# Stick-breaking and dilated scores: the second query tile as three rounded float32r terms, and the stick-breaking work moved along the projection chunks

## The chip, the cores and the metric

The kernel runs on one core of a Trainium2 chip. The metric is the time of one execution on the device in microseconds; the median of three runs before the change is 249.99 us (249.98 to 250.0). A core has TensorE (matmuls; PE in the profile, PEld its weight loads), VectorE (DVE), ScalarE (ACT), GpSimd (POOL) and SyncE (SP), each with its own instruction queue that it works off in order, 16 DMA engines, the on-chip memory SBUF, and PSUM, eight banks into which TensorE writes. GpSimd cannot read PSUM.

## The reference, cut to what matters

Two layers of a decoder trunk, over 256 positions (two tiles of 128) of width 1024. Each layer normalises x, projects it to ten groups of columns, runs three branches over heads of width 64, gates them, and adds the output projection to x:

```python
hn = rms_norm(x, norm_gain)
proj = einsum('bsd,de->bse', hn, w_in)
a_q, a_k, a_v, a_g, b_x, b_g, c_q, c_k, c_v, c_g = split(proj)
qa, ka = rope(a_q), rope(a_k)                    # 8 heads
y_a = dilated_attention(qa, ka, va) * silu(a_g)
y_b = rg_lru_branch(b_x, ...) * silu(b_g)        # conv of width 4, then a gated recurrence
y_c = stick_breaking_attention(qc, kc, vc) * silu(c_g)   # 4 heads
x = x + einsum('bse,ed->bsd', concat([y_a, y_b, y_c]), w_out)
```

Dilated attention takes the causal scores q.k, weights them by how many of three (window, dilation) patterns hold a key, and applies a softmax. Stick-breaking takes z = q.k/8 under a strict causal mask, and weighs key s by sigmoid(z_s) times the product of sigmoid(-z_j) over the keys j between s and the query. Both need, per head, the scores of query tile 0 against keys 0 to 127 and of query tile 1 against keys 0 to 255. All is float32, and the output is compared in float32.

## The kernel before, in words

**Precision.** Projections are done in three terms. Each float32 operand is split into a rounded high part (type float32r) and a low part, the difference, also rounded; the product is high.high + low.high + high.low, with three float32r matmuls. The weights arrive by DMA in chunks (`load_chunk`, L101 to L111): per chunk two transfers on SP's queue, four ScalarE copies that round (L109), four VectorE subtracts that give the low part (L110). Scores, in contrast, are plain float32 matmuls before the change (L443 for stick-breaking, L497 for dilated), which TensorE works off as two records (passes) each.

**Order.** TensorE's order is the order of the program text (`manual_schedule` for TensorE). On the other engines a planner decides at build time in which order each queue holds its instructions; it goes by dependencies, the program order as priority, and its own estimate of times. Chunks are asked for `AHEAD` = 2 chunks in front of the one in use, 1 where the chunk has work placed in its middle, with the second then asked for behind that work (`proj_b`, L314 to L346).

The projection chunks that matter run in this order in each layer: CQ, CK (stick-breaking q and k), AQ0, AK0 (dilated q and k of heads 0 to 3), BX (recurrence input), AQ1, AK1 (dilated heads 4 to 7), CG (stick-breaking gate), BG, AG. A chunk is two halves of 128 output columns. In layer 0 each half is 24 matmuls of 256 columns (L211). In layer 1 the chunks CQ to AK1 are "paired": 8 matmuls of 512 columns that carry high and low part of x at once (L332) and 8 of 256 (L329), and ScalarE and VectorE then add the two halves of the result (L335, L337).

Other work is placed between halves, by the argument `mid` of `proj_b`. Before the change:

- mid AQ0: the stick-breaking scores (`sb_scores`, L436), then on ScalarE two sigmoids per head, on VectorE two scans and a product per head (L454, L456);
- behind AQ0 and AK0: their results are rotated (`rotate`, L476: four VectorE instructions each) into the tiles q0 and k0;
- mid BX and behind BX: the 12 transposes of the stick-breaking weights (`turned`, L458 to L464), one bank and then two; behind BX also the convolution on VectorE and two small DMAs on GpSimd's queue (L549);
- mid AQ1: the first dilated scores (`dil_scores(0)`, L489) and their softmax: VectorE masks and takes the extreme value (L504), ScalarE exponentiates (L514), VectorE divides (L517);
- behind CG: the transposes of those probabilities; mid BG: the recurrence's gate matmuls (L557), both products with v (L427) and the second dilated scores (`dil_scores(4)`).

**Buffers.** Scores and transposes share four PSUM banks (`at`), projections three (`pp`). A head of 64 lies on partitions 0 to 63 or 64 to 127, so heads come in pairs that use different rows of TensorE's array. The SBUF tiles named yh0, yl0 (first half of the gated outputs, split), ag (dilated gate) and q0 have one buffer each: a new use waits until all readers of the last one are done. GpSimd does little: memsets of a column of the stick-breaking weights (L452), small scalars, two DMAs per layer.

Of the kernel before, what the change touches and what calls it, by code (L numbers as in the profile page):

```python
# [9 lines left out]
F32 = mybir.dt.float32  # L10
# [38 lines left out]
def trunk_kernel(ctx: ExitStack, tc: tile.TileContext, x, first_x, first, wpack, prm_d, gatew, gains, consts, rope, out):  # L49
# [247 lines left out]
    for l in range(L):  # L297
# [7 lines left out]

        y_half(0)

        def proj_a(ps, w, t, kb, nk, cw, first, last):
# [125 lines left out]
        halves = ((0, slice(0, 128)), (1, slice(128, 384)))  # L434

        def sb_scores():  # L436
            for p in (0, 2):
                for h in (p, p + 1):
                    zs[h] = bank(at, "s")
                for t, cs in halves:  # L440
                    for h in (p, p + 1):
                        hr, hb, _ = head(h)
                        pe.matmul(zs[h][:, cs], qc[hr, hb, t * P:(t + 1) * P], kc[hr, hb, 0:(t + 1) * P],  # L443
                                  start=t == 0, stop=True, skip_group_check=True)
            table(SIGM, [split[l, CH_AK[0]]])
            for h in range(NHC):
                z = zs[h][:, 0:384]
                bt, om = scr(384), scr(384)
                tab(om, z, AF.Sigmoid, scale=-1.0)
                tab(bt, z, AF.Sigmoid)  # L450
                w = sw[h] = wk.tile([P, 384], F32, name="sw", tag="sw", bufs=4)
                gps.memset(w[:, 127::256], 0.0)  # L452
                for lo, n in ((0, 127), (128, 255)):
                    dve.tensor_tensor_scan(w[:, lo:lo + n][:, ::-1], om[:, lo + 1:lo + 1 + n][:, ::-1],  # L454
                                           diag[:, 255 - n:255][:, ::-1], 0.0, ALU.mult, ALU.add)
                dve.tensor_mul(w, bt, w)  # L456
# [32 lines left out]
        def dil_scores(h0):  # L489
            sps = {}  # L490
            for p in (h0, h0 + 2):
                for h in (p, p + 1):
                    sps[h] = bank(at, "s")
                for t, cs in halves:
                    for h in (p, p + 1):
                        hr, hb, _ = head(h - h0)
                        pe.matmul(sps[h][:, cs], qT[h0][hr, hb, t * P:(t + 1) * P], kT[h0][hr, hb, 0:(t + 1) * P],  # L497
                                  start=True, stop=True)
            shifted = {}
            for h in range(h0, h0 + 4):  # L500
                xs = scr(384)
                mn = wk.tile([P, 2], F32, name="mn", tag="mn", bufs=4)
                for t, cs in halves:
                    dve.tensor_tensor_reduce(xs[:, cs], sps[h][:, cs], nmask[:, cs], -0.125, 3e38,  # L504
                                             ALU.add, ALU.min, mn[:, t:t + 1])
# [30 lines left out]
        bg = sb.tile([P, 2, S], F32, name="bg", tag="bg")  # L536
        ag = sb.tile([P, 4, S], F32, name="ag", tag="ag")
        cg = sb.tile([P, 2, S], F32, name="cg", tag="cg")
# [87 lines left out]
        emit_y(rt, bg, 0, 2)  # L626
        dil_softmax(y_c["s"])
        ps = proj_b(CH_AG)
        table(SIGM)
# [146 lines left out]
```

## Time and profile before

| | |
|---|---|
| median of three runs | 249.99 us (249.98 to 250.0) |
| the profiled execution's own time | 248.82 us |
| its span, first to last instruction | 246.7 us |
| granted TensorE clock | 0.996 |
| busy: TensorE, VectorE, ScalarE, GpSimd | 97%, 80%, 68%, 5% of the span |
| float32 score matmuls, records of 256 columns (L443 and L497) | 16 and 32, 377 ns each |
| float32 score matmuls, records of 128 columns | 16 and 32, 296 and 297 ns each |
| projection matmuls, float32r, 256 columns (L211, input whi) | 480, 285 ns each |

A row of a group reads: line, engine, operation, output<-inputs, shape, count, then busy time and the mean duration of one in ns, then idle time before them and what ended it. A record's duration holds its pipeline latency too; what one record costs in a stream is the distance from start to start. A row of the chain or of a timeline begins with the start and the length in us from the start of the span; a timeline row can hold a run of several instructions, with their count.

### The profile page before, as it was taken

What the parts mean: (1) busy time and instruction counts of PE and PEld (TensorE: products, weight loads), DVE (VectorE), ACT (ScalarE), POOL (GpSimd) and SP (SyncE); (2) the same over time, 40 slices, a digit from 0 to 9 for tenths busy, and PEclk for the clock granted to TensorE, in tenths of its full rate; (3) what the DMA queues carried; (4) which work ended last, traced back from release to release, by engine and by line L of the source; (5) the groups of instructions that cost most, each with busy time, mean ns of one, the idle gap of its engine ahead of it and who ended that gap; (6) DMA issues with size and microseconds to landing.
All of it is one profiled execution on the core that took longest, in us unless ns stands there. A gap on an engine that the chain in (4) does not pass through costs nothing.

```text
span 246.7 us, 4531 instructions
## 1 busy us (share of the span) xinstructions
PE 239.0 (97%) x1657; PEld 212.1 (86%) x1657; DVE 196.5 (80%) x442; ACT 167.2 (68%) x360; POOL 12.1 (5%) x45
## 2 busy tenths in 40 slices
PE   8999999999999999999999999999999999999990
PEld 4889999999998899878889988889889889987870
DVE  3885699999999799985792766999999987985253
ACT  3778989735947499964662885865498649992142
POOL 0037000001000000000100000000010000000000
PEclk9999999999999999999999999999999999999998
DMA  6989889268447741277157486605553672000022
GB/s 201 404 292 403 342 288 333 96 215 268 134 157 255 258 117 56 85 240 284 74 189 232 142 268 243 200 7 165 161 157 119 197 262 98 0 0 3 0 85 85
DMA packets 13173, 43.89 MB, mean 178 GB/s; under 512 B 1632, under 2 KB 2144, under 8 KB 13152
## 3 DMA queue, kind: packets, MB, share of 16 engines
q1 hardware_dynamic: 12384, 42.30, 51.1%
q10 hardware_dynamic: 576, 0.79, 0.9%
q0 software_dynamic: 192, 0.52, 0.7%
q8 instruction: 13, 0.21, 0.4%
q14 instruction: 8, 0.07, 0.1%
HBM read 42.03 MB, written 1.05 MB: 175 GB/s over the span
## 4 chain that ended last, share of the span: by engine, by line
PE 94%; DMA 2%; DVE 1%; ACT 1%; SPq 0%; issue 0%; ACTq 0%
PE pp L211 51%; PE pp L332 11%; PE s L211 9%; PE pp L329 5%; PE s L169 4%; PE s L463 3%; PE s L497 2%; PE y L427 2%; DMA st<-first 2%; PE pp L169 2%; PE s L443 1%; PE pp L427 1%; PE s L557 1%; PE s L259 1%; DVE xres L668 0%; ACT scr L242 0%
## 5 line engine op out<-in xcount | busy, mean ns | idle before, releaser
L110 DVE TENSOR_TENSOR wlo<-st,whi 128x512 fp32r<-128x512 f32 x132 | 84.1, 683 | 12.8 <-ACT whi L109 12.5
L109 ACT ACTIVATE whi<-st 128x512 fp32r<-128x512 f32 x132 | 73.9, 629 | 28.0 <-PE pp L211 11.8
L211 PE MATMUL pp<-xx,whi 128*128 128x256 f32 x480 | 63.3, 285 | 0.0
L211 PEld LDWEIGHTS pp<-xx,whi 128*128 128x128 f32 x480 | 59.7, 191 | 1.4 <-issue 1.3
L211 PE MATMUL pp<-xx,wlo 128*128 128x256 f32 x240 | 33.7, 283 | 0.0
L211 PEld LDWEIGHTS pp<-xx,wlo 128*128 128x128 f32 x240 | 30.9, 192 | 0.0
L332 PE MATMUL pp<-xx,whi 128*128 128x512 f32 x112 | 29.3, 396 | 0.0
L332 PEld LDWEIGHTS pp<-xx,whi 128*128 128x128 f32 x112 | 20.1, 189 | 4.1 <-ACT scr L83 0.3
L77 ACT ACT_TABLE_LOAD x13 | 16.7, 1283 | 1.9 <-PEq L769 1.7
L83 ACT ACTIVATE pr<-scr,mn 128x128 f32<-128x128 f32 (+1 forms) x32 | 14.1, 442 | 5.2 <-DVE mn L504 5.2
L329 PEld LDWEIGHTS pp<-xx,wlo 128*128 128x128 f32 x112 | 15.3, 190 | 1.1
L329 PE MATMUL pp<-xx,wlo 128*128 128x256 f32 x112 | 15.6, 282 | 0.0
L211 PE MATMUL pp<-whi,yh 128*128 128x512 f32 x48 | 14.5, 403 | 0.0
L211 PE MATMUL pp<-wlo,yh 128*128 128x512 f32 x48 | 14.0, 393 | 0.0
L211 PE MATMUL pp<-whi,yl 128*128 128x512 f32 x48 | 14.0, 393 | 0.0
L335 ACT ACTIVATE low<-pp 128x256 f32<-128x256 f32 x14 | 5.3, 382 | 9.1 <-PE pp L332 6.8
L211 PEld LDWEIGHTS pp<-wlo,yh 128*128 128x128 f32 x48 | 9.0, 188 | 2.1
L211 PEld LDWEIGHTS pp<-whi,yl 128*128 128x128 f32 x48 | 9.0, 188 | 2.0
L211 PEld LDWEIGHTS pp<-whi,yh 128*128 128x128 f32 x48 | 8.6, 188 | 2.0 <-issue 0.3
L169 PE MATMUL s<-whi,xx 128*128 128x512 f32 (+1 forms) x36 | 10.2, 404 | 0.1
L415 ACT ACTIVATE yh<-scr 128x512 fp32r<-128x512 f32 x8 | 5.0, 631 | 7.7 <-DVE scr L413 7.6
L504 DVE CUSTOM_DVE_ANT_0 scr<-s,con 128x128 f32<-128x128 f32 (+1 forms) x32 | 9.2, 351 | 0.0
(165 smaller groups left out, 355.2 us busy)
## 6 DMA issues: line engine op xcount, KB each, us to landing
st<-w_pack SPq DMA_DIRECT2D x66, 512.0 KB, 5.4
st<-first SPq DMA_DIRECT2D x7, 512.0 KB, 6.2
xres<-x_in SPq DMA_DIRECT2D x2, 512.0 KB, 8.1
gw_t<-gate_w SPq DMA_DIRECT2D x2, 256.0 KB, 6.9
gn<-gains SPq DMA_DIRECT2D x1, 512.0 KB, 6.7
xs<-xc POOLq DMA_DIRECT2D x4, 128.0 KB, 3.7
gf<-gains SPq DMA_DIRECT2D x1, 512.0 KB, 6.8
out<-scr SPq DMA_DIRECT2D x2, 256.0 KB, 2.1
```

What stands on the lines that cost most here:

```text
L77: load = act.preload_act_table_set(name)
L83: i = dep(act.activation(*a, **k), loaded["load"])
L109: split[l, c] = act.activation(hi[:, ws], st[:, ss], AF.Copy)
L110: dve.tensor_sub(lo[:, ws], st[:, ss], hi[:, ws].bitcast(F32))
L169: pe.matmul(ps[t][:, c0 - base:c1 - base], a[:, k, t * P:(t + 1) * P], b[:, c0:c1], start=k == 0 and i == 0 and c0 == base, stop=k == NK - ...
L211: pe.matmul(ps, a(k), b(k), start=first and i == 0, stop=last and i == len(seq) - 1)
L329: pe.matmul(ps[:, 0:S], lo[:, k, cs], xh[:, k, :], start=False, stop=False, skip_group_check=True)
L332: pe.matmul(ps, hi[:, k, cs], xx[:, k].rearrange("p h t -> p (h t)"), start=i == 0, stop=i == len(seq) - 1, skip_group_check=True)
L335: act.activation(low, ps[:, S:2 * S], AF.Copy, scale=sc)
L427: pe.matmul(y[hr, p * 128 + o:p * 128 + 256], vt[:, s0, hs], wts[i][s0], start=s0 == 0, stop=s0 == 1)
L463: pe.transpose(tp[:, i * P:(i + 1) * P], tiles[h0 + h][:, j * P:(j + 1) * P], ident)
L504: dve.tensor_tensor_reduce(xs[:, cs], sps[h][:, cs], nmask[:, cs], -0.125, 3e38, ALU.add, ALU.min, mn[:, t:t + 1])
```

## The change: what it does

For query tile 1 of all score groups, the float32 matmul is replaced by three float32r matmuls over rounded parts: q high . k high, q low . k high, q high . k low, summed in PSUM. Query tile 0 stays float32. A new function `split_keys` makes the parts: for q's second tile a copy that rounds and a subtract on GpSimd; for k over all 256 keys a copy on ScalarE (on GpSimd for heads 4 to 7) and a subtract on GpSimd. The parts live in the tiles yh0 and yl0 (stick-breaking, then heads 0 to 3) and ag and q0 (heads 4 to 7), so the gated outputs' first half and the gate tile are allocated later. A new function `scores` issues the matmuls, for each pair of heads: tile 0, then the three terms.

The stick-breaking scores move from the middle of AQ0 to the middle of AK0, their transposes from the middle and end of BX to the middle and end of AK1. BX has nothing in its middle any more. In layer 1 the first dilated scores move from the middle of AQ1 to its end; in layer 0 they stay.

```diff
-        y_half(0)
-
+        exact = {}
+
+        def split_keys(h0, q, k, tags):
+            parts = []
+            for full, tag, n in ((q[:, :, P:S], tags[1], P), (k, tags[0], S)):
+                both = sb.tile([P, 2, 2, n], F32R, name="qk3", tag=tag)
+                hi, lo = both[:, 0], both[:, 1]
+                if n == S and h0 != 4:
+                    act.activation(hi, full, AF.Copy)
+                else:
+                    gps.tensor_copy(hi, full)
+                gps.tensor_sub(lo, full, hi.bitcast(F32))
+                parts.append((hi, lo))
+            (qh, ql), (kh, kl) = parts
+            exact[h0] = (qh, kh), (ql, kh), (qh, kl)
+
+        def scores(ps, h0, q, k, p):
+            for n, (a, b) in enumerate(((q, k), *exact[h0])):
+                cs = slice(0, P) if n == 0 else slice(P, 384)
+                for h in (p, p + 1):
+                    hr, hb, _ = head(h)
+                    pe.matmul(ps[h][:, cs], a[hr, hb, 0:P], b[hr, hb, 0:P if n == 0 else S],
+                              start=n < 2, stop=n in (0, 3), skip_group_check=True)
+
         def sb_scores():
...
-                for t, cs in halves:
-                    for h in (p, p + 1):
-                        hr, hb, _ = head(h)
-                        pe.matmul(zs[h][:, cs], qc[hr, hb, t * P:(t + 1) * P], kc[hr, hb, 0:(t + 1) * P],
-                                  start=t == 0, stop=True, skip_group_check=True)
+                scores(zs, "sb", qc, kc, p)
...
         def dil_scores(h0):
...
-                for t, cs in halves:
-                    for h in (p, p + 1):
-                        hr, hb, _ = head(h - h0)
-                        pe.matmul(sps[h][:, cs], qT[h0][hr, hb, t * P:(t + 1) * P], kT[h0][hr, hb, 0:(t + 1) * P],
-                                  start=True, stop=True)
+                scores(sps, h0, qT[h0], kT[h0], p)
...
-        ag = sb.tile([P, 4, S], F32, name="ag", tag="ag")
...
             proj_to(kc, CH_CK)
+        split_keys("sb", qc, kc, ("yh0", "yl0"))
...
-        rotate(proj_b(CH_AQ[0], sb_scores), qT, 0, "q0")
-        rotate(proj_b(CH_AK[0]), kT, 0, "k0")
-        sw_t, sw_heads = turned_tile()
-        conv(lambda: turned(sw, 0, (0,), sw_t))
-        turned(sw, 0, (1, 2), sw_t)
+        rotate(proj_b(CH_AQ[0]), qT, 0, "q0")
+        rotate(proj_b(CH_AK[0], sb_scores), kT, 0, "k0")
+        split_keys(0, qT[0], kT[0], ("yh0", "yl0"))
+        conv(None)
...
-        rotate(proj_b(CH_AQ[1], second), qT, 4, "q1")
-        rotate(proj_b(CH_AK[1]), kT, 4, "k1")
+        q1_ps = proj_b(CH_AQ[1], second if l == 0 else None)
+        if l > 0:
+            second()
+        rotate(q1_ps, qT, 4, "q1")
+        sw_t, sw_heads = turned_tile()
+        rotate(proj_b(CH_AK[1], lambda: turned(sw, 0, (0,), sw_t)), kT, 4, "k1")
+        turned(sw, 0, (1, 2), sw_t)
+        split_keys(4, qT[4], kT[4], ("ag", "q0"))
...
         silu(cg, cg_ps)
 
+
+        y_half(0)
...
         dil_softmax(y_c["s"])
+        ag = sb.tile([P, 4, S], F32, name="ag", tag="ag")
         ps = proj_b(CH_AG)
```

More of the change, by code (lines that the diff above doesn't have):

```diff
@@ L490, in dil_scores @@
             sps = {}
-            for p in (h0, h0 + 2):
+            for p in (0, 2):
                 for h in (p, p + 1):
                     sps[h] = bank(at, "s")
-                for t, cs in halves:
-                    for h in (p, p + 1):
-                        hr, hb, _ = head(h - h0)
-                        pe.matmul(sps[h][:, cs], qT[h0][hr, hb, t * P:(t + 1) * P], kT[h0][hr, hb, 0:(t + 1) * P],
-                                  start=True, stop=True)
+                scores(sps, h0, qT[h0], kT[h0], p)
             shifted = {}
@@ L503, in dil_scores @@
                 for t, cs in halves:
-                    dve.tensor_tensor_reduce(xs[:, cs], sps[h][:, cs], nmask[:, cs], -0.125, 3e38,
+                    dve.tensor_tensor_reduce(xs[:, cs], sps[h - h0][:, cs], nmask[:, cs], -0.125, 3e38,
                                              ALU.add, ALU.min, mn[:, t:t + 1])
```

## The prediction

> **What bounds the kernel now.** I read the page's busy shares first, then the chain of waits in order of time, then the groups of instructions by shape, then the timelines of VectorE and GpSimd around the moved stages.
>
> ```profile
> PE 239.0 (97%) x1657; PEld 212.1 (86%) x1657; DVE 196.5 (80%) x442; ACT 167.2 (68%) x360; POOL 12.1 (5%) x45
> ...
> PE 94%; DMA 2%; DVE 1%; ACT 1%; SPq 0%; issue 0%; ACTq 0%
> ```
>
> TensorE is 94% of the chain. In order of time its pieces touch one another through both layers, so a microsecond taken from TensorE's work is a microsecond off the end, and a wait put before a matmul is added in full. The pieces that the change touches (start, length, what; the x counts records):
>
> ```profile
> 31.23 0.45 PE y L379 x4
> ...
> 37.43 1.51 PE s L443 x16
> 38.94 11.71 PE pp L211 x96
> 50.66 0.44 PE s L463 x4
> 51.09 2.88 PE pp L211 x24
> 53.98 0.88 PE s L463 x8
> 54.85 2.86 PE pp L211 x24
> 57.72 1.51 PE s L497 x16
> 59.23 14.59 PE pp L211 x120
> 73.82 1.32 PE s L463 x12
> ...
> 78.01 1.02 PE s L557 x16
> ...
> 175.25 1.51 PE s L497 x16
> ...
> 191.10 1.32 PE s L463 x12
> ```
>
> There are six score groups (three per layer), 1.51 us each. A float32 matmul leaves two records (passes): 4 heads x 2 query tiles x 2 = 16. Half a projection chunk of 24 rounded (float32r) matmuls with 256 columns takes 2.88 us, 0.12 us each.
>
> The second bound is VectorE, which is full in the stage where the change works:
>
> ```profile
> core 0: us, PE busy (x) PEld busy (x) DVE busy (x) ACT busy (x) POOL busy (x), PEclk, DMA share, GB/s
> 31.00:56.00 25.00, 25.00 (x214) 24.49 (x214) 24.56 (x48) 18.43 (x35) 0.41 (x4) 1.00 0.70 234
> 56.00:81.00 25.00, 25.00 (x229) 23.41 (x229) 24.92 (x68) 17.30 (x43) 1.25 (x2) 1.00 0.64 204
> ```
>
> It does this without making TensorE wait, since much of it is splitting weights ahead of need; the granted clock is 1.00, so no clock effect enters the sum.
>
> **The score matmuls.** Inside the first group, records in flight at four moments (start, length, run):
>
> ```profile
> 37.68 0.39 PE L443 MATMUL s<-kc,qc 64*128 64x256 f32 x2
> ...
> 38.12 0.39 PE L443 MATMUL s<-kc,qc 64*128 64x128 f32 x4
> 38.23 0.50 PE L443 MATMUL s<-kc,qc 64*128 64x128 f32 x4
> ```
>
> Records come in pairs, the two heads of a pair on 64 partitions each. Two slots of 256 columns lie between 37.68 and 38.12, 0.22 us each; one of 128 columns between 38.12 and 38.23, 0.11. So the second tile costs 2 passes x 2 pairs x 0.22 = 0.88 us of the group's 1.51. The change replaces it by 3 terms x 2 pairs. No row shows a rounded matmul on 64 partitions. The nearest slot is the projection's 0.12 for 256 columns: 6 x 0.12 = 0.72, a gain of 0.16 per group. Bounds: at best the 0.11 of a record that streams 128 columns in float32, 6 x 0.11 = 0.66, gain 0.22; at worst the pairs do not run side by side, 12 x 0.12 = 1.44, a loss of 0.56. I take 0.12, since float32 records of the same partitions pair in every group. Six groups: **-0.96 us** (bounds -1.32 and +3.36). The first tile's matmuls, the entry and the exit of the group stay.
>
> **The splits.** Each of three calls per layer rounds q's second tile (copy and subtract, 256 columns, GpSimd) and all of k (512 columns: copy on ScalarE, on GpSimd for the second head group; subtract on GpSimd): per layer 3 + 3 instructions of 256 and 3 + 1 of 512 on GpSimd, 2 on ScalarE. ScalarE's is a row of the page, 0.63 us, and ScalarE is busy 18.43 of 25. GpSimd has only narrow rows:
>
> ```profile
> L195 DVE TENSOR_SCALAR ss<-sq x2: 154/154/155, 22.0 to 23.5; 128x1 f32<-128x1 f32 x2
> L195 POOL TENSOR_SCALAR ss<-sq x2: 181/524/867, 116.5 to 122.6; 128x1 f32<-128x1 f32 x2
> ...
> L109 ACT ACTIVATE whi<-st 128x512 fp32r<-128x512 f32 x132 | 73.9, 629 | 28.0 <-PE pp L211 11.8 <-DMA st<-w_pack 10.9 <-PE s L211 4.9
> L110 DVE TENSOR_TENSOR wlo<-st,whi 128x512 fp32r<-128x512 f32 x132 | 84.1, 683 | 12.8 <-ACT whi L109 12.5
> L337 DVE TENSOR_TENSOR scr<-pp,low 128x256 f32<-128x256 f32 x8 | 3.3, 418 | 0.0
> ```
>
> VectorE's 0.68 us (512) and 0.42 (256) bound it below. Above: the same narrow operation takes 524 ns on GpSimd and 154 on VectorE in the mean, 3.4 times: 2.3 and 1.4. I take 1.2 and 0.6: undisturbed the ratio is only 181/154 = 1.2, so 0.8 and 0.5, and the rest is for waiting behind VectorE, which the next rows show.
>
> ```profile
> 18.34 0.22 POOL L285 TENSOR_SCALAR ls<-ls 128x4 f32<-128x4 f32 x1
> 18.46 1.29 DVE L110 TENSOR_TENSOR wlo<-st,whi 128x512 fp32r<-128x512 f32 x2 [1.05 <-ACT whi L109]
> 18.64 0.57 POOL L284 TENSOR_TENSOR ls<-ls,ls 128x4 f32<-128x4 f32 x1
> 19.30 0.54 POOL L285 TENSOR_SCALAR ls<-ls 128x4 f32<-128x4 f32 x1
> 19.92 0.20 POOL L284 TENSOR_TENSOR ls<-ls,ls 128x4 f32<-128x4 f32 x1
> ```
>
> A GpSimd operation of 0.20 takes 0.54 to 0.57 if it starts inside a VectorE subtract, and ends just behind it (19.84, the second subtract at 19.75). The other direction, VectorE behind a wide GpSimd operation, no row shows: it costs VectorE between nothing and GpSimd's whole time; I take the whole time. The Trainium skill ("SBUF — State Buffer", Who interferes with whom) says the pair of ports is held for a whole instruction, whoever comes first; the trace agrees in the direction it has, 0.57 against 0.20. The Trainium skill ("GPSIMD Engine Reference", 3.1) gives a wide two-input operation 1.96 times VectorE's time, an estimate of 1.34 and 0.82 us; no row here shows it, and by it the wait worked out below would be 0.9 and the time 249.9.
>
> **The tight place: the first dilated scores in layer 0.** VectorE before:
>
> ```profile
> 38.84 1.00 DVE L454 TENSOR_TENSOR_SCAN sw<-scr,con 128x127 f32<-128x127 f32 x2 [0.44 <-ACT scr L83]
> ...
> 44.43 0.55 DVE L456 TENSOR_TENSOR sw<-scr,sw 128x384 f32<-128x384 f32 x1
> ...
> 49.75 0.74 DVE L481 STREAM_SHUFFLE scr<-pp 128x512 f32<-128x512 f32 x1
> ...
> 52.18 0.69 DVE L484 TENSOR_TENSOR k<-k,scr 128x512 f32<-128x512 f32 x1
> ```
>
> The stick-breaking scores move one chunk (two halves of 2.88): from 37.43 to 43.19. VectorE's scans, ahead of the key's rotation in its queue, then end at 44.98 + 5.76 = 50.7 instead of 44.98. Rotating k takes 49.75 to 52.87, 3.1: it ends at 53.9, where before it ended 4.9 before the scores at 57.72. Then ScalarE's copy 0.63, the subtract 1.2 and two handovers of about 0.1: k's low part stands at 55.9. TensorE now comes to these scores sooner, since the transposes (0.44 + 0.88) that lay before them move behind: 57.72 - 1.32 - 0.16 = 56.2; the term with k's low part is the fourth round, behind about 0.56 us of others: 56.8. Spare 0.9. But q's split (2 x 0.6) must wait for the buffer that the stick-breaking scores free at 44.6, so it falls among the scans and holds VectorE 1.2 us: 57.1. **A wait of 0.3 us.** Behind the waiting matmul stands the rest of TensorE's queue, in order.
>
> **What I cost at nothing.** Stick-breaking's own split in layer 0: k is scaled as early as before, and the scores move from 37.43 to 43.19, 5.8 us for 1.2 + 0.63 + 1.2. Layer 1: the first dilated scores stand behind the whole chunk, and the half chunk more (2.8) covers the split; without it the same wait comes again. There the softmax has less time: scores start at 175.25 + 2.8 - 1.3 - 0.2 = 176.6 and the transposes come at about 190.8. Layer 0 shows what is needed:
>
> ```profile
> L517 DVE TENSOR_SCALAR pr<-pr,den x8: 277/314/347, 63.6 to 65.9; 128x128 f32<-128x128 f32 x4, 128x256 f32<-128x256 f32 x4
> ```
>
> from 57.72 to 66.3, 8.6 of 14.2 us. Stick-breaking's transposes lie inside that stretch in both layers; their count stays, and their weights are done by 51 to 52 and read at about 63. The second head group's split has from about 70 to the scores behind 78.01. On GpSimd's queue the layer 1 memsets, which wait for the moved transposes, go from about 51-55 to 63-67; behind them may stand the two gate DMAs, which are needed only at the gate matmuls (78.01). The weights keep their order; a chunk is asked for up to one place sooner or later, and SP's queue issues the same transfers. GpSimd's wide work, 6 x 0.6 + 4 x 1.2 = 8.4 us a layer, can push VectorE's weight splits back as far; the look-ahead of two chunks (11.5 us) hides it. Without that, each microsecond counts.
>
> **The sum.** -0.96 + 0.3 = -0.66 us: from the profiled execution's 248.82 (span 246.7 and 2.1 around it) to 248.2, and from the median of the runs, 249.99, to **249.35**. The median lies 1.2 above the profiled execution; I carry the difference over as it is.
>
> **The rivals.** *The gain is eaten at the tight place.* GpSimd at 0.9 and 1.6, between its bounds: k's low part at 53.9 + 1.8 + 0.83 + 1.6 = 58.1, a wait of 1.3, time 250.3. For it: VectorE has nothing spare from 31 to 81. Against it: its queue may turn the key sooner than behind the interleaved weight subtract (0.6 in the 3.1).
>
> *GpSimd blocks VectorE, slower.* Place: the same. At 1.4 and 2.3: 53.9 + 2.8 + 0.83 + 2.3 = 59.8, a wait of 3.0, time 252.0. It makes the kernel slower once the wait passes 1.5, about 1.0 and 1.7 us per operation. For it: the mean row (524 against 154). Against it: that row is narrow and mostly waiting.
>
> *The rounded terms do not cost what I take*, so that the change doesn't do what it says: unpaired, 253.4; paired, but at the 0.22 of float32 slots, 6 x 0.22 - 0.88 = +0.44 a group, 252.6. For it: no row on 64 partitions. Against: pairs everywhere, and 0.12 in all projections.
>
> **How the numbers follow.** Chances: the forecast 0.42 (own range 248.7 to 249.5), the eaten gain 0.30, the block 0.22, the terms 0.06. 248.7 is -1.32 without a wait; 251.6 leaves out the dearest half of the block, the terms, and a little below, under 0.2 in all. A measurement of this kernel tells about 0.2%, 0.5 us, from no change. Faster by more than that (under 249.49): nearly all of the forecast, 0.40. Within: the eaten gain and the forecast's edge, 0.32. Slower: block and terms, 0.28.
>
> **What would show it.** In the chain, score groups of 1.35 instead of 1.51, with pairs of rounded 256-column records 0.12 apart. A gap of TensorE before the third term in layer 0's first dilated group, released by GpSimd: 0.3 if right, over 1.3 by the rivals. GpSimd's subtracts of 512 columns at 1.2, and VectorE standing still during them. No wait before layer 1's. Wrong: a group over 1.51, or TensorE waiting for weight halves or for the transposes' probabilities.

## The result, and the profile after

The changed kernel takes **255.82 us** (median of four runs, 255.57 to 256.98) beside 249.99 us for the kernel before: a ratio of 1.0248, with a 95% interval of 1.0214 to 1.0282. It is 2.5% slower, and 255.82 lies outside the predicted range of 248.7 to 251.6. Its profiled execution took 255.93 us with a span of 254.1 and a granted clock of 0.993. Two of the four executions of run e7 below took 260.74 and 261.55 us at a lower granted clock (0.982 and 0.979), and its median is that of the other two, 255.51 and 257.11.

The page of the changed kernel, first the busy time of the engines, then the chain that ended last, then two groups (busy time, mean ns of one, idle time before them):

```profile
PE 240.5 (95%) x1681; PEld 212.9 (84%) x1681; DVE 205.1 (81%) x442; ACT 169.6 (67%) x364; POOL 34.1 (13%) x65
...
PE 42%; DVE 34%; DMA 11%; ACT 6%; issue 4%; SPq 1%; ACTq 0%; DVEq 0%
...
L110 DVE TENSOR_TENSOR wlo<-st,whi 128x512 fp32r<-128x512 f32 x132 | 91.1, 736 | 11.4 <-ACT whi L109 11.2
...
L445 POOL TENSOR_TENSOR qk<-k,qk 128x512 fp32r<-128x512 f32 x4 | 6.6, 1659 | 20.5 <-ACT qk L442 20.3
```

TensorE was 94% of the chain before; now it is 42%, and VectorE is 34%. VectorE executes as many instructions as before (442), yet is busy 205.1 us instead of 196.5: its weight subtract (L110) takes 736 ns in the mean instead of 683. GpSimd's busy time rose from 12.1 to 34.1 us. The four 512-column GpSimd subtracts of the last row take 1.66 us in the mean.

The view of waits of the changed kernel, TensorE's alone (who waited for what: us in total, times, longest):

```profile
PE s L481 <- DVE mn L518: 1.5, 1, 1.5
PE s L455 <- POOL qk L445: 1.5, 1, 1.5
...
PE s L570 <- ACT pa L482: 1.2, 1, 1.2
...
PE s L211 <- ACT yh L413: 0.7, 1, 0.7
```

The kernel before has none of these. Only the second is the one that was predicted, and it is five times as long. In the order of the run: layer 0's first dilated scores wait for k's low part (57.6 to 59.4 us of the span); layer 0's out projection waits for the gated outputs of the recurrence (100.6 to 101.6); layer 1's stick-breaking transposes wait until VectorE has masked the dilated scores that hold their PSUM bank (184.7 to 186.6); layer 1's gate matmuls wait for an eviction on ScalarE (201.1 to 202.6).

The score groups themselves became what was forecast. TensorE's timeline of the changed kernel through the first stick-breaking group (start, length, instruction, count):

```profile
44.09 0.49 PE L455 MATMUL s<-kc,qc 64*128 64x128 f32 x4
44.34 0.61 PE L455 MATMUL s<-qk,qk 64*128 64x256 f32 x6
44.77 0.39 PE L455 MATMUL s<-kc,qc 64*128 64x128 f32 x4
44.91 0.61 PE L455 MATMUL s<-qk,qk 64*128 64x256 f32 x6
45.45 0.74 PE L211 MATMUL pp<-xx,whi 128*128 128x256 f32 x4
```

From 44.09 to 45.45 the group takes 1.36 us; it was 1.51. The three pairs of rounded records of the first two heads take 0.43 us (44.34 to 44.77): behind the first comes the second after 0.20, and from there on they are 0.12 apart, as in the projections. Four of the six groups take 1.35 to 1.37 us.

To compare traces, the time from the first float32r projection (L211) to the end of the span is used below and called the **rest**, because the first transfers land earlier or later from execution to execution. It was 224.28 us before and is 231.01 now: +6.73. Taking TensorE's distances from start to start apart by kind of matmul, the six score groups give +1.15 (two waits and six gains), the gate matmuls +2.25, the paired projections with the bank wait behind them +1.57, the other projections with the wait for the out projection +1.17, and everything else 0.6 in small pieces.

### The profile page after: what moved, and what is told of

Same layout as the page of the kernel before. It is cut to its first block, busy times and chain, and to the rows that moved or that the text cites. A ratio compares the mean times of both kernels' runs of the same rounds, so it can differ in the third digit from the quotient of the medians.

```text
span 254.1 us, 4604 instructions
## 1 busy us (share of the span) xinstructions
PE 240.5 (95%) x1681; PEld 212.9 (84%) x1681; DVE 205.1 (81%) x442; ACT 169.6 (67%) x364; POOL 34.1 (13%) x65
## 4 chain that ended last, share of the span: by engine, by line
PE 42%; DVE 34%; DMA 11%; ACT 6%; issue 4%; SPq 1%; ACTq 0%; DVEq 0%
PE pp L211 21%; DVE wlo L110 10%; PE s L211 9%; DMA st<-w_pack 5%; PE pp L330 4%; DMA xres<-x_in 3%; DVE sw L472 3%; DMA st<-first 3%; DVE scr L518 2%; DVE xc L559 2%; PE pp L327 2%; PE y L425 2%; DVE sw L474 2%; DVE scr L499 1%; DVE pr L531 1%
## 5 line engine op out<-in xcount | busy, mean ns | idle before, releaser
L110 DVE TENSOR_TENSOR wlo<-st,whi 128x512 fp32r<-128x512 f32 x132 | 91.1, 736 | 11.4 <-ACT whi L109 11.2
L211 PE MATMUL pp<-xx,whi 128*128 128x256 f32 x480 | 63.6, 285 | 0.0
L211 PEld LDWEIGHTS pp<-xx,whi 128*128 128x128 f32 x480 | 59.6, 191 | 0.8 <-ACT whi L109 0.2
L211 PE MATMUL pp<-xx,wlo 128*128 128x256 f32 x240 | 33.7, 283 | 0.0
L211 PEld LDWEIGHTS pp<-xx,wlo 128*128 128x128 f32 x240 | 31.0, 192 | 0.0
L211 PE MATMUL pp<-whi,yh 128*128 128x512 f32 x48 | 14.5, 405 | 0.0
L211 PE MATMUL pp<-whi,yl 128*128 128x512 f32 x48 | 14.1, 396 | 0.0
L211 PE MATMUL pp<-wlo,yh 128*128 128x512 f32 x48 | 14.1, 395 | 0.0
L211 PEld LDWEIGHTS pp<-whi,yl 128*128 128x128 f32 x48 | 9.0, 188 | 2.2
L211 PEld LDWEIGHTS pp<-wlo,yh 128*128 128x128 f32 x48 | 9.0, 188 | 2.2
L211 PEld LDWEIGHTS pp<-whi,yh 128*128 128x128 f32 x48 | 8.6, 188 | 2.1 <-DVE wlo L110 0.2
L445 POOL TENSOR_TENSOR qk<-k,qk 128x512 fp32r<-128x512 f32 x4 | 6.6, 1659 | 20.5 <-ACT qk L442 20.3
```

The source lines that it names most:

```text
L110: dve.tensor_sub(lo[:, ws], st[:, ss], hi[:, ws].bitcast(F32))
L211: pe.matmul(ps, a(k), b(k), start=first and i == 0, stop=last and i == len(seq) - 1)
L445: gps.tensor_sub(lo, full, hi.bitcast(F32))
```

## The experiments

| run | what it is | median us | ratio to before, 95% | rest us | VectorE busy us | mean L110 ns |
|---|---|---|---|---|---|---|
| before, first profile | | 249.99 | | 224.28 | 196.5 | 683 |
| after | the change | 255.82 | 1.0248, 1.0214 to 1.0282 | 231.01 | 205.1 | 736 |
| e14 | the kernel before again | 249.70 | 0.9996, 0.9976 to 1.0015 | 224.28 | 196.3 | 682 |
| e1 | the moves alone | 251.46 | 1.0063, 1.0043 to 1.0083 | 226.42 | 195.9 | 684 |
| e2 | moves and terms, no splits | 251.52 | 1.0052, 1.0034 to 1.0071 | 226.01 | 196.3 | 684 |
| e11 | and the rounding copies | 251.45 | 1.0080, 1.0052 to 1.0109 | 225.78 | 197.6 | 693 |
| e13 | and copies for the subtracts | 252.77 | 1.0101, 1.0060 to 1.0142 | 228.10 | 201.1 | 710 |
| e3 | moves and splits, no terms | 258.11 | 1.0301, 1.0242 to 1.0359 | 233.73 | 205.7 | 738 |
| e8 | e3 with memsets for the splits | 251.76 | 1.0073, 1.0044 to 1.0102 | 226.31 | 197.1 | 685 |
| e4 | splits on ScalarE and VectorE | 252.48 | 1.0089, 1.0067 to 1.0111 | 226.97 | 201.6 | 682 |
| e5 | terms and splits, places of before | 253.17 | 1.0136, 1.0097 to 1.0175 | 227.84 | 205.7 | 748 |
| e9 | places of before, dilated terms, no GpSimd | 252.01 | 1.0080, 1.0050 to 1.0109 | 226.36 | 199.9 | 686 |
| e6 | e1, ScalarE's order changed | 250.44 | 1.0030, 1.0007 to 1.0052 | 226.70 | 196.2 | 686 |
| e7 | after, ScalarE's order changed | 256.31 | 1.0277, 1.0235 to 1.0318 | 231.59 | 204.1 | 727 |
| e10 | e1 less one move | 250.70 | 1.0056, 1.0033 to 1.0079 | 225.47 | 196.0 | 684 |
| e12 | e9 and relief for VectorE | 251.16 | 1.0065, 1.0041 to 1.0088 | 225.42 | 196.4 | 684 |
| e15 | before and relief for VectorE | 249.65 | 0.9984, 0.9967 to 1.0001 | 224.28 | 193.0 | 685 |

Medians are device times; rest, busy time and mean are of the one profiled execution of each. L110 is the line of VectorE's weight subtract (L111 in e7 and e8). A ratio is taken against runs of the kernel before on the same chip.

### The parts of the change one by one: e1, e2, e3

**e1, the moves alone.** Everything stays where the change puts it, but `split_keys` returns at once and all scores are float32.

```diff
         def split_keys(h0, q, k, tags):
-            parts = []
...
+            return
...
-            for n, (a, b) in enumerate(((q, k), *exact[h0])):
+            for t, cs in halves:
```

> The changed kernel with its new places, but all scores as float32 matmuls of the kernel before and no splits (the output stays the reference's). Theory A (GpSimd's wide operations hold VectorE up, and its lateness reaches TensorE in four places): without them none of the four waits is left, 249.5 to 250.5 us. Theory B (the new places alone are too late, the splits only add the first wait): the waits before layer 1's stick-breaking transposes (1.9 us) and before its gate matmuls (1.5) stay, 253 to 254 us.

Measured: 251.46 us, 1.0063. Its view of waits has one line for TensorE that the kernel before has not:

```profile
PE s L558 <- ACT pa L470: 1.1, 1, 1.1
```

The time lies between the two theories. The moves, which the prediction took as free, cost 1.4 us. In the trace the rest is 2.14 us longer, and a wait before layer 1's gate matmuls, a gap of 1.43 us from start to start, is most of it.

**e2, moves and terms without splits.** The rounded parts are slices of xh and xl, which stand ready.

```diff
-            parts = []
...
+            kh, kl = xh[:, 0:2, :], xl[:, 0:2, :]
+            qh, ql = xh[:, 2:4, 0:P], xl[:, 2:4, 0:P]
             exact[h0] = (qh, kh), (ql, kh), (qh, kl)
```

> The changed kernel, but the rounded parts are slices of the split x that is there anyway: no split of q and k is computed, so the scores of the second query tile are of other numbers. It has the new places and the rounded matmuls on 64 partitions. Theory A: 249.0 us, six groups at 1.35 instead of 1.51 us and no waits. Theory B: 252 to 253 us, the two late waits stay.

Measured: 251.52 us, 1.0052. All six groups take 1.353 to 1.364 us, so the terms themselves give 0.92 us. The median doesn't show it, because the same wait has grown (view of waits of e2):

```profile
PE s L561 <- ACT pa L473: 1.7, 1, 1.7
```

From start to start the gap is 2.08 us instead of 1.43: TensorE arrives earlier at a place whose time is set by another engine. The rest falls by 0.41 only, from 226.42 to 226.01.

**e3, splits that nobody reads.** The splits are computed as in the change, the scores are float32.

```diff
         def scores(ps, h0, q, k, p):
-            for n, (a, b) in enumerate(((q, k), *exact[h0])):
+            for t, cs in halves:
```

> The changed kernel with all splits computed on GpSimd and ScalarE, but nothing reads them: the scores are the float32 matmuls of before. Theory A: the wait for k's low part in layer 0 (1.6 us) goes, the other three stay, and the matmuls give back 1.0: 254 to 255.5 us. Theory C (what costs is that TensorE waits for the low part, and the later waits are its echo): 250 to 251 us.

Measured: 258.11 us, 1.0301, above both forecasts. No matmul waits for a split here, since none reads one, and still the loss is there: the interval of the ratio overlaps the change's. That it looks larger proves little: the four executions lie between 255.41 and 258.95 us. In the profiled one, the longest, the granted clock fell to a half for 3.4 us behind a wait, and the products with v in that stretch took 4.17 us instead of the 2.75 of e1. So it is not the latency of k's low part that costs 6 us, but what the splits do to the engines beside them. VectorE's busy time, 205.7 us, is that of the change, and so is its weight subtract, 738 ns. The row of that subtract, and two lines of the view of waits of e3:

```profile
L110 DVE TENSOR_TENSOR wlo<-st,whi 128x512 fp32r<-128x512 f32 x132 | 91.4, 738 | 13.7 <-ACT whi L109 13.5
```

```profile
PE s L569 <- ACT pa L481: 3.0, 2, 2.2
PE s L480 <- DVE mn L517: 1.3, 1, 1.3
```

The waits for the masks and before layer 1's gates stand there as in the change, the gates of layer 0 have one of 0.8 besides, and the wait before layer 0's out projection is missing.

### Which engine, and what it is that holds VectorE up: e4, e8, e11, e13

**e4, no GpSimd.** Copies on ScalarE, subtracts on VectorE.

```diff
-                if n == S and h0 != 4:
-                    act.activation(hi, full, AF.Copy)
-                else:
-                    gps.tensor_copy(hi, full)
-                gps.tensor_sub(lo, full, hi.bitcast(F32))
+                act.activation(hi, full, AF.Copy)
+                dve.tensor_sub(lo, full, hi.bitcast(F32))
```

> The changed kernel with every copy of the splits on ScalarE and every subtract on VectorE, nothing on GpSimd. Adds 3 x 0.68 + 3 x 0.42 = 3.3 us of work per layer to VectorE instead of GpSimd's 8 us beside it. Theory A with a full block (VectorE loses what GpSimd takes): clearly better than the change, 250 to 253 us, since VectorE loses less. Theory D (GpSimd and VectorE share little; VectorE is simply full, so any added lateness shows): 255 us or more, as VectorE has more to do than in the change.

Measured: 252.48 us, 1.0089, as theory A had it. The weight subtract is back at 682 ns and VectorE's busy time at 201.6 us, 5 of which are the new subtracts; the waits before layer 1's gates and transposes are gone. One wait of some size is left, in layer 0 (view of waits of e4):

```profile
PE s L211 <- ACT yh L413: 0.9, 1, 0.9
```

**e8, memsets of the same busy time.** e3, with every wide GpSimd operation replaced by three memsets (`REP` = 3) of its output; no low part is computed, and ScalarE's copies stay.

```diff
-                both = sb.tile([P, 2, 2, n], F32R, name="qk3", tag=tag)
+                both = sb.tile([P, 2, 2, n], F32, name="qk3", tag=tag)
...
-                    gps.tensor_copy(hi, full)
-                gps.tensor_sub(lo, full, hi.bitcast(F32))
+                    for _ in range(REP):
+                        gps.memset(hi, 0.0)
+                for _ in range(REP):
+                    gps.memset(lo, 0.0)
```

> As the kernel whose splits nothing reads (ratio 1.0301), but each wide GpSimd operation is replaced by three memsets of the same shape, which write and read nothing; the splits are not computed. Theory A (the block comes from GpSimd reading SBUF beside VectorE's instructions with two SBUF inputs): VectorE's weight subtracts stay at 0.68 us in the mean and the time is that of the moves alone, 251 to 252 us. Rival (any GpSimd work holds VectorE up, or GpSimd's queue being full delays something): 254 us or more.

Measured: 251.76 us, 1.0073. Two lines of its page, the busy times and the weight subtract (L111 in this kernel):

```profile
PE 240.6 (96%) x1657; PEld 212.7 (85%) x1657; DVE 197.1 (79%) x442; ACT 169.3 (68%) x364; POOL 32.7 (13%) x105
...
L111 DVE TENSOR_TENSOR wlo<-st,whi 128x512 fp32r<-128x512 f32 x132 | 84.2, 685 | 11.5 <-ACT whi L110 11.0
```

GpSimd is as busy as in e3 (32.7 against 32.2 us), and VectorE isn't touched: 685 ns. Being busy is not what hurts; GpSimd's operations that read SBUF do. The time is that of the moves alone, and so is the wait that is left, 1.0 us before layer 1's gates (1.1 in e1).

**e11, the copies without the subtracts**, and **e13, a copy in the place of each subtract.** The instructions of TensorE are those of the change in both. The first added line is e11's, the second e13's.

```diff
-                gps.tensor_sub(lo, full, hi.bitcast(F32))
+                lo = xl[:, 0:2, 0:n]
+                gps.tensor_copy(lo, full)
```

> The changed kernel without the six subtracts per two layers' splits: all rounding copies stay on ScalarE and GpSimd, but the low parts are slices of x's low part, so the terms with a low part are scores of other numbers; the instructions of TensorE are the same. It leaves out the low parts of q and k. GpSimd's wide work falls from about 21 to about 8 us. Theory (the loss grows with the GpSimd time that reads SBUF beside VectorE): 252.5 to 253.5, the mean subtract of weights at 700 to 715 ns, between the 684 of the moves alone and the 736 of the change. Rival (the loss is the one wait for k's low part and its consequences): 251.3 to 251.8, as with no splits at all.

> The changed kernel with each GpSimd subtract replaced by a GpSimd copy of its first input, of the same size and at the same place; it leaves out the low parts of q and k (the terms with a low part are scores of other numbers). All GpSimd work then reads one input. Theory (it is the subtracts' two inputs that hold up VectorE): the weights' subtract at 690 to 705 ns, VectorE's busy time 198 to 200 us, 251.4 to 252.5 us. Rival (any wide reading does): 720 to 740 ns, 203 to 205 us, 254 to 256.

Measured: 251.45 us, 1.0080, and 252.77 us, 1.0101. Their weight subtracts, from the page of e11 and then of e13:

```profile
L110 DVE TENSOR_TENSOR wlo<-st,whi 128x512 fp32r<-128x512 f32 x132 | 85.4, 693 | 11.9 <-ACT whi L109 11.6
```

```profile
L110 DVE TENSOR_TENSOR wlo<-st,whi 128x512 fp32r<-128x512 f32 x132 | 87.6, 710 | 11.8 <-ACT whi L109 11.7
```

VectorE's busy time over e2 rises by 1.3 us with the 8 GpSimd copies, by 4.8 with 20, and by 8.8 with 8 copies and 12 subtracts. e11's time came out at the rival's figure (no more than without splits) and its mean subtract short of the theory's 700 to 715. e13 falls between its two forecasts: 710 ns and 252.77, just above the theory's 705 and 252.5 and far from the rival's. So one-input operations hold VectorE up as well, but 12 two-input ones cost it twice what 12 copies do (7.5 against 3.5 us). Whether that is their second input or only their longer time, these runs don't separate. What they do show is that the step from 252.8 to 255.8 is the subtracts'.

### The places: e5, e9, e10

**e5, places of before.** The three terms and the GpSimd splits are added to the kernel before, each split behind the stage that makes its inputs; nothing else moves.

```diff
-                for t, cs in halves:
-                    for h in (p, p + 1):
...
+                scores(zs, "sb", qc, kc, p)
...
+        split_keys("sb", qc, kc, ("yh0", "yl0"))
```

> The changed kernel with its three terms and its splits on GpSimd, but every score group and every transpose at the place of the kernel before. Theory A (what GpSimd takes from VectorE is the main cost, wherever the scores stand): 254 to 257 us, with a wait of 2 us or more before layer 0's stick-breaking scores, because k's low part then comes after them. Theory B' (the moves are a main cost): 252 to 253 us or less.

Measured: 253.17 us, 1.0136: between the two forecasts, and better than the change by some 2.6 us, at about the same load of VectorE (205.7 us, 748 ns). The moves, made to give the splits time, cost more than the waits that they avoid: without them the wait for GpSimd is 0.3 us in the view of waits, at the stick-breaking scores of layer 0, where 2 us or more were forecast.

**e9, dilated terms only, at the places of before, without GpSimd.** e4's split, for the two dilated calls, in e5.

```diff
-                scores(zs, "sb", qc, kc, p)
+                for t, cs in halves:
...
-        split_keys("sb", qc, kc, ("yh0", "yl0"))
```

> The places of the kernel before, stick-breaking scores in float32 as before, and the three terms for the dilated scores alone (four groups), with every copy of their splits on ScalarE and every subtract on VectorE. If the four groups give 0.155 us each and the splits fit into the 3 to 8 us that the keys have to spare there: 249.4 us. If VectorE's added 2.2 us per layer reach TensorE by the weights or the recurrence: 250 to 251.5 us.

Measured: 252.01 us, 1.0080, above both forecasts. VectorE has 3.4 us more work in all, and TensorE waits 0.8 for layer 0's out projection and 0.3 for layer 0's gates. The smallest version of the idea loses too.

**e10, one move undone.** e1, with layer 1's first dilated scores in the middle of AQ1 again.

```diff
-        q1_ps = proj_b(CH_AQ[1], second if l == 0 else None)
-        if l > 0:
-            second()
+        q1_ps = proj_b(CH_AQ[1], second)
```

> The moves alone with float32 scores and no splits (251.46 us, 1.0063), but layer 1's first dilated scores stay in the middle of AQ1 as before. Theory (the 1.4 us wait before layer 1's gate matmuls in the moves alone comes from that later softmax): the wait is gone and 249.9 to 250.2. Rival (it comes from the transposes moved to AK1, whose evictions push ScalarE's copies): the wait stays and 251.2 to 251.7.

Measured: 250.70 us, 1.0056. In the trace the gap before the gates falls from 1.43 to 0.61 us and the rest from 226.42 to 225.47, but the median stands between the two forecasts and the interval of the ratio overlaps e1's. The later softmax is a part of that wait; how large a part of the moves' cost stays open.

### The order of ScalarE's queue: e6, e7

The chain that ended last in the changed kernel, in order of time, just ahead of layer 1's gate matmuls (start, length, what):

```profile
193.86 1.82 DVE wlo L110 x3
...
195.73 4.63 DMA st<-w_pack
...
202.08 0.50 ACT pa L482
...
202.62 0.43 PE s L570
```

VectorE's subtracts free a staging buffer at 195.7, the next transfer into it takes 4.63 us, ScalarE copies it, and only then comes, in ScalarE's queue, the eviction of the transposes (L482) that frees the gates' PSUM bank. A transfer that nobody needs yet is in the path because of the order of one queue. In e6 (from e1) and e7 (from the change, whose lines then stand one further down) ScalarE's copies of the out projection's first chunk of weights (CH_O) are put behind the evictions. The edit of e7, to which e6's comes down as well:

```diff
                 split[l, c] = act.activation(hi[:, ws], st[:, ss], AF.Copy)
+                if c == CH_O: dep(split[l, c], turn_last["i"])
...
-                act.activation(to[g], tp, AF.Copy)
+                turn_last["i"] = act.activation(to[g], tp, AF.Copy)
```

> The kernel with the new places and float32 scores (median 251.46, ratio 1.0063), with one edit: the first two of ScalarE's rounding copies of the output chunk, which wait for a weight transfer, stand behind the evictions of the probabilities' transposes in ScalarE's queue instead of ahead of them. Theory E (those copies hold up the evictions, and so the gate matmuls, by 1.4 us, and that is all that the moves cost): 249.8 to 250.3 us and no wait before the gate matmuls. Rival (TensorE would wait for VectorE's lateness in another place): 251 us or more, the wait turns up elsewhere.

> The changed kernel whole, with one ordering edit: the first two ScalarE copies of the weights of chunk CH_O are put behind the evictions of the dilated transposes on ScalarE's queue, so that the gate's exponential no longer stands behind a copy that waits for a transfer. Theory (the 1.5 us wait of TensorE before layer 1's gate matmuls, at 201.06 in the changed kernel, is paid by that order alone): the wait goes, and 254.2 to 254.8. Rival (the splits are late whatever the order of that queue, since VectorE frees the staging buffers late; the wait turns up at the next place): 255.3 to 256, with a wait of about 1 us within the following 10 us.

Measured: e6 250.44 us, 1.0030; e7 256.31 us, 1.0277. The wait before the gates is gone in both. In e6 that brings, by the ratios, about half of what the moves cost, though the two intervals overlap. Its trace, of the longest of its ten executions (252.09 us), shows no gain: the rest is 226.70 against 226.42. Of this 0.9 us lie in the first projections, at 29 to 31 us, far ahead of the edited place. But 1.2 us are a wait that turned up again, as the rival had it: 4 us behind the gates the second dilated scores take 2.67 us instead of 1.51, since the gates' operations on ScalarE, which free the PSUM banks for these scores, stand behind two rounding copies whose transfer lands at 200.25. In e7 the time isn't better, and the rival is right again: the wait turns up within 5 us, twice as long. The timeline of e7 there, all engines:

```profile
201.26 4.91 DVE L111 TENSOR_TENSOR wlo<-st,whi 128x512 fp32r<-128x512 f32 x8
...
201.31 6.59 POOL L446 TENSOR_TENSOR qk<-k,qk 128x512 fp32r<-128x512 f32 x1
...
204.72 0.49 PE L456 MATMUL s<-qk,qk 64*128 64x256 f32 x4
...
206.68 0.70 DVE L412 TENSOR_TENSOR scr<-y,cg 128x512 f32<-128x512 f32 x1
...
207.96 0.39 PE L456 MATMUL s<-qk,qk 64*128 64x256 f32 x2 [2.75 <-POOL qk L446]
208.13 0.69 DVE L415 TENSOR_TENSOR yl<-scr,yh 128x512 fp32r<-128x512 f32 x1 [0.76 <-ACT yh L414]
```

Read it from the top: GpSimd's subtract of k starts at 201.31, just behind the start of a VectorE operation. VectorE then runs ten two-input operations back to back until 207.38 and isn't slowed (0.70 each). GpSimd ends at 207.90: 6.59 us for an operation that takes 1.3 at its best in the changed kernel. That is 1.22 us behind the start of L412, the only one of the ten that has one of its inputs in PSUM (y); the nine before it read both from SBUF. k's subtract of layer 0 in the changed kernel, shown further down, likewise ends 1.20 us behind the start of L390, which reads pp from PSUM. So it seems that GpSimd came through when VectorE read only one input from SBUF; no run tests that by itself. TensorE, ahead of the third term, waits for it from 204.9 to 207.96.

### The kernel before as a yardstick, and an attempt to beat it: e14, e12, e15

> The kernel before, unchanged, to have a second profiled execution of it. Theory (its first profiled execution, 248.82 us, was 1.2 us under the median because the first transfers landed early there, which let the first projection start at 22.43): a profiled execution near 250, with that start at 23.2 to 23.7 and the rest, from there to the end, within 0.3 of the 224.28 us of the first. Rival (the rest varies): a rest of 225 or more.

Measured: 249.70 us. The start of the first float32r projection in the timeline of the kernel before, its first profile and then e14:

```profile
22.43 1.84 PE L211 MATMUL pp<-xx,whi 128*128 128x256 f32 x14
```

```profile
23.30 0.88 PE L211 MATMUL pp<-xx,whi 128*128 128x256 f32 x6
```

From there to the end it is 224.28 us in both. Of the 1.2 us by which the first profile lay under the median, 0.87 were the landing of the first transfers; carrying the difference over was right. The other 0.3 lie within the spread of the executions (249.14 to 250.25).

**e12** gives some of VectorE's work to ScalarE in e9; **e15** does the same in the kernel before.

```diff
-                for t, cs in halves:
-                    dve.tensor_scalar(pr[:, cs], pr[:, cs], den[:, t:t + 1], None, ALU.mult)
+                act.activation(pr[:, 0:128], pr[:, 0:128], AF.Copy, scale=den[:, 0:1])
+                dve.tensor_scalar(pr[:, 128:384], pr[:, 128:384], den[:, 1:2], None, ALU.mult)
...
-                dve.tensor_scalar(xc[:, b, :], bxp[:, b, 3:259], prm[:, b, 3:4], prm[:, b, 4:5], ALU.mult, ALU.add)
+                act.activation(xc[:, b, :], bxp[:, b, 3:259], AF.Identity, scale=prm[:, b, 3:4], bias=prm[:, b, 4:5])
```

> The places of before, three terms for the dilated scores only, copies on ScalarE and subtracts on VectorE (252.01 us), with some 2.9 us of VectorE's work per layer given to ScalarE: the first operation of the convolution and the division of the first query tile's probabilities. Theory (the terms pay as soon as VectorE isn't asked for more time than before): four groups at 1.36, no wait for the recurrence or the gates, 249.3 to 249.8, under the kernel before. Rival (ScalarE's chain before the out projection or the gates becomes the late one): 250.5 to 252, with waits released by ScalarE.

> The kernel before with the same 2.9 us per layer given from VectorE to ScalarE (the first operation of the convolution, the division of the first query tile's probabilities), float32 scores. Theory (the relief itself is late at layer 0's gate matmuls, where the kernel with terms and relief waited 0.9 us): 250.4 to 251.2, with a wait before those gates. Rival (the terms' subtracts are late there): no wait, 249.3 to 249.9.

Measured: e12 251.16 us, 1.0065, within its rival's range; e15 249.65 us, 0.9984 (0.9967 to 1.0001, not told apart from before). In e15, as its rival had it, no wait appears, VectorE is busy 3.5 us less and the rest is 224.28 again: with VectorE in time, more slack on it is worth nothing. In e12 VectorE's load is that of the kernel before and the wait for the out projection is gone, but a wait of 0.5 us for ScalarE before layer 0's gates is left, and ScalarE has gone from 167.2 to 177.1 us. The relief alone doesn't make that wait (e15), and neither is it all of e12's loss: its rest is 1.1 us longer in spite of four cheaper groups. What the remainder is stays open. No version tried beats the kernel before.

## Why the prediction was wrong, point by point

- **What bounds the kernel: right.** e15 takes 3.5 us from VectorE and TensorE's rest doesn't move; the gaps that the change puts before matmuls lengthen the rest.
- **The score matmuls: right.** 1.35 forecast, 1.352 to 1.365 measured where no wait falls into the group, paired on 64 partitions; 0.92 us in all in e2, for the 0.96 of the sum. The rival of dear terms is out.
- **The base: right** but for 0.3 us (e14).
- **The size of the GpSimd operations: too small.** 1.2 and 0.6 were taken; the page gives 1.66 and 1.44 for the two groups of 512-column subtracts, 1.09 and 0.90 for those of 256, 0.89 and 1.01 for the copies of 256 and 512. The wide work is 23 us in all, 11.5 a layer and not 8.4. These means lie within the bounds that were drawn, but the bounds don't hold for single operations: a copy of 256 columns takes 1.91 at 194.0 us of the changed kernel (the bound was 1.4), and e7 has a subtract of 6.59 (2.3). The Trainium skill ("GPSIMD Engine Reference", 3.1), whose factor gave an estimate of 1.34 and 0.82 us, was nearer, and close to the shortest that the trace shows, 1.29 and 0.74. The 512-column subtracts of k in the view of that line (shortest, median and longest in ns):

```profile
L445 POOL TENSOR_TENSOR qk<-k,qk x4: 1294/1606/2130, 57.2 to 200.8; 128x512 fp32r<-128x512 f32 x4
```

- **The tight place: the place right, 0.3 us predicted, 1.5 measured.** The timeline of the changed kernel, all engines:

```profile
55.70 0.68 DVE L502 TENSOR_TENSOR k<-k,scr 128x512 f32<-128x512 f32 x1
...
56.30 1.88 DVE L110 TENSOR_TENSOR wlo<-st,whi 128x512 fp32r<-128x512 f32 x3
56.47 0.63 ACT L442 ACTIVATE qk<-k 128x512 fp32r<-128x512 f32 x1 [2.68 <-DVE k L502]
...
57.16 0.49 PE L455 MATMUL s<-k,q 64*128 64x128 f32 x4
57.18 2.13 POOL L445 TENSOR_TENSOR qk<-k,qk 128x512 fp32r<-128x512 f32 x1 [9.86 <-ACT qk L442]
...
57.40 0.49 PE L455 MATMUL s<-qk,qk 64*128 64x256 f32 x4
58.11 0.68 DVE L390 SCALAR_TENSOR_TENSOR bxp<-pp,rb 128x512 f32<-128x512 f32 x1
58.71 1.15 DVE L110 TENSOR_TENSOR wlo<-st,whi 128x512 fp32r<-128x512 f32 x1
59.37 0.39 PE L455 MATMUL s<-qk,qk 64*128 64x256 f32 x2 [1.48 <-POOL qk L445]
```

  k is rotated at 56.38, where 53.9 plus q's 1.2 made 55.1; this execution's first projection starts 0.7 later than that of before (23.14 against 22.43), so VectorE was 0.6 late on its own. The copy (0.63) is as forecast. The subtract of k is the term that was mis-sized: 2.13 for 1.2, and it ends while a VectorE operation beside it takes 1.15 instead of 0.68. Together that is 1.5 of lateness (0.6 and 0.9), less 0.3 because the scores came later too (57.16 against 56.2 plus the same 0.7), on top of the forecast 0.3. The rivals at this place had 1.3 and 3.0: the measured wait is that of the eaten gain, which alone would have ended near 250.3.
- **The step that failed is "What I cost at nothing".** It holds two claims. One was that GpSimd's work can push VectorE back only as far as the look-ahead of weights hides. The weights were indeed in time: no wait of TensorE names a weight half. But VectorE's queue is in order, and the lateness hits whatever else stands in it: the masks that free PSUM banks in layer 1 (1.5), the end of the recurrence in layer 0 (0.7 by the view of waits), and the staging buffers, so that the next transfers, ScalarE's copies of them and the eviction queued behind these copies come late (1.2 by that view). e3 shows the first and the last of the three (1.3 and 2.2) with no score reading a split. e8, with memsets, shows only the 1.0 before the gates that the moves alone have as well. The other claim was that the moved transposes and the later layer 1 scores cost nothing "in that stretch": e1 measures 1.4 us for the moves alone.
- **VectorE behind GpSimd**: the prediction said that no row shows it, and took GpSimd's whole time for VectorE's loss. Measured, the loss is 8.8 us over e2, some 40% of GpSimd's 23. The size was on the safe side; the wrong part was to charge it at one place (q's 1.2) and to look for its end only there. The Trainium skill ("SBUF — State Buffer", Who interferes with whom) has the ports held for whole instructions by whoever comes first. The traces agree that one engine stands while the other works, in both directions: 1.15 for 0.68 on VectorE in the timeline above, 6.59 for 1.3 on GpSimd in e7. They don't agree on who goes first: in e7 eight VectorE operations with both inputs in SBUF, which by the trace start after GpSimd's, went ahead of it.
- **The range** was drawn from one place only. The slower case had 0.28, 0.22 of it for a GpSimd that blocks VectorE and is late at that place. That the two engines stand in each other's way is what happened, but the wait at that place was that of the eaten gain, and the rest of the loss came at three other places, at one of which the moves alone wait as well (e1).

## What to carry to other kernels

Work put on an idle engine isn't free if it holds up an engine that is nearly full, as GpSimd's reads of SBUF did here: price it on that neighbour's queue, and follow everything that stands in that queue, not only the item that the work feeds. When an engine in order is full, a look-ahead for one kind of its work says nothing about the others; list the deadline of each. A gain on the bounding engine is only collected if whatever it meets next is early as well: in e2, 0.92 us of true gain in the score groups became 0.41 in the trace, and none in the median, because TensorE came sooner to a wait.

## What the runs showed of the hardware that was not expected

- A GpSimd subtract of 512 columns can be starved: 6.59 us (e7), while nine VectorE operations with both inputs in SBUF ran back to back and kept their 0.70 us each, against 1.3 to 2.1 us for the same operation in the changed kernel. It ended 1.22 us behind the start of the next VectorE operation, which reads PSUM.
- GpSimd memsets with the same busy time (32.7 us) leave VectorE's operations as they were (685 against 684 ns); copies lengthen them (693 and 710), subtracts more (736).
- In e3 a wait of 2.2 us before layer 1's gates was followed by a low granted clock, in the stretch from 204 to 212 us; e7's wait of 2.75 us was not (1.00 from 204 to 220). What decides is open. The row of e3 (stretch, length, busy time of PE, PEld, DVE, ACT, POOL, granted clock, DMA share, GB/s):

```profile
204.00:212.00 8.00, 8.00 (x70) 5.59 (x69) 7.24 (x18) 4.74 (x11) 0.00 (x0) 0.79 0.77 253
```
